# Own tiles for pieces and differences in attention's sums, and one load and one store for the block differences of the token stage

## The chip, the cores and the metric

The kernel runs on one core of a Trainium2 chip. The metric is the device time of one execution in microseconds (us), shown as the median of several runs. A profile of one execution shows what each engine did: PE is TensorE (matmuls), DVE is VectorE, ACT is ScalarE, POOL is GpSimd, and SP is SyncE, which here does nothing but issue transfers. A transfer (a DMA) is issued by an engine's queue in that queue's order and lands some microseconds later.

## The reference

One step of a one-layer encoder in float32, for a prompt of 2048 tokens and a sample of 32 tokens with 1024 cached keys. The input is normalised and modulated to h; one projection gives the columns of two branches; a sparse attention (an indexer picks up to 256 keys for each query) and a gated short convolution are merged by gates and projected:

```python
h = rms_norm(x, norm_g) * (1.0 + scale[:, None, :]) + shift[:, None, :]
proj = h @ w_in
(q, k, v, za, qi, ki, wi, u, bg, cg, zb, ga, gb) = jnp.split(proj, ...)
...
_, idx = lax.top_k(score, topk)          # score: indexer, qi . ki, weighted by wi
o = softmax(q . k[idx] / sqrt(d)) @ v[idx]
a_out = (o * jax.nn.silu(za)) @ w_pa
b_out = (bg * conv3(cg * u) * jax.nn.silu(zb)) @ w_pb
merged = jax.nn.sigmoid(ga) * a_out + jax.nn.sigmoid(gb) * b_out
y = x + gate[:, None, :] * (merged @ w_out)
```

The change touches how h and b (the input of `w_pb`) are stored and differenced; what is computed stays the same.

## The kernel before

Every f32 operand is split in two parts, hi and lo (`split`, L194: hi is a cast on ACT, lo a subtraction on DVE or POOL), and each product is three matmuls. The large products use seven block products in place of eight, on the quadrants of an operand (two halves of its 1024 channels, two halves of its tokens) and on differences of these. The differences are made ahead of time and stored in device memory.

**Token stage** (0 to about 274 us of the profile). `mk_h` normalises and transposes pairs of 128-token tiles, makes h, and stores it to `h_d` (L701). The projections that are needed per token (indexer, k, v; matmuls L813 to L815) run at the same time; their results are stored from ACT's queue. In the second half of the stage the block differences of h are made in 12 pieces, 3 chunks of tokens (352, 352, 336 of a half) by 4 slabs of 128 channels, at the steps listed in `SUMS_AT`. `sums_load` (L710) loads the four quadrants of a piece into a tile `hv` by two transfers (L715), one for each channel half; `block_sums` (L719) makes four differences in place on DVE (L724) and stores them with two transfers to `t_d` (L726). The tile has two buffers. The loads and the differences are kept in program order.

**Feature stage** (about 285 to 1750 us). `b_piece` (L1028) loads four slabs of h from `h_d`, or of differences from `t_d`, into `ev` tiles (L1037, seven buffers) and splits them; `mm` multiplies with the split weights `wo` (L1051 to L1053), which come from `wr` (L988). The indexer's scores (transposes L243 of a query tile `qd` that is loaded by L236 and L237, then matmuls L256, L267, L268 and L287) are woven in.

**Attention** (about 1745 to 2290 us). Blocks of 128 queries run in the order 4, 0, 5, 1, 6, 2, 7, 3, 8 to 15. `qk` makes scores (matmuls L1461 to L1463), masks them on DVE (L1472) and takes the exponential on ACT (L1477); `pv` transposes them (L1498), splits them (tiles `th`, `tl`) and multiplies with v (L1506 to L1508); z is loaded by L1513, multiplied in on DVE (L1515, L1516), and the result is stored by L1521. Keys and values are loaded two tiles at a time as the blocks need them (L1393, tile `in`) and split into `khi`, `klo`, `vhi`, `vlo`; queries by L1433, masks by L1426.

From the fifth block of that order on, **side work** is handed out by `sum_steps` (L1282): 32 pieces of b (load L1295 from `b_d`, four subtractions on POOL L432, store L1308 to `xb_d`), one piece for the sample, and 24 sums of weights (load L1328, four POOL operations L1332, store L1335 to `o_d`). All of them use one tag `wq` of 4 KB per partition with two buffers. A piece of b takes its first half for the input and its second half for the differences:

```python
st["t"] = tile_()
load(st["t"][:, :512].rearrange("p (k t) -> p k t", k=2), ...)
...
o = st["t"][:, 512:].rearrange("p (s b t) -> p s b t", s=4, t=64)
```

The step list issues the load of piece i+1 ahead of the subtractions of piece i. Since a tile is free only when everything that reads it is done, the load of piece i+2 waits until the store of piece i has landed.

What sets the order: nearly all loads and stores are issued by SP, in one in-order queue (`load = store = nc.sync.dma_start`); a transfer whose condition isn't met holds all that are queued behind it. The order of the instructions within each engine is decided by the framework's scheduler when the kernel is built, from program order and priorities, except where `tc.keep_in_program_order` fixes it. Transfers share eight semaphores (lanes) in turn, and a transfer waits, beside its data, for an earlier one on its lane. A pool opened with `reuse_waits="tile"` takes over memory of closed pools with waits for the tiles that lay there, and a pool without it with waits for the engines that used the memory.

Of the kernel before, what the change touches and what calls it, by code (L numbers as in the profile page):

```python
# [9 lines left out]
F32 = mybir.dt.float32  # L10
# [4 lines left out]
ALU = mybir.AluOpType  # L15
# [4 lines left out]
P = 128  # L20
D = 1024
KT = 8
SEQ = 2048
# [3 lines left out]
NTOK = SEQ + NS  # L27
NB = 16
HT = NTOK // 2
CHUNKS = [(0, 352), (352, 352), (704, 336)]  # L30
# [79 lines left out]
def body(ctx, tc, x_prompt, x_sample, cache_k, cache_v, cache_idx_k, state_conv, c_prompt, c_sample,  # L110
# [3 lines left out]
    V, S, G, T = nc.vector, nc.scalar, nc.gpsimd, nc.tensor  # L114
    load = nc.sync.dma_start
    store = nc.sync.dma_start
# [3 lines left out]
    def nm(s):  # L120
        uid[0] += 1
        return f"{s}_{uid[0]}"
# [10 lines left out]
    dp = ctx.enter_context(tc.tile_pool(name="dp", bufs=1, space=DRAM))  # L133
# [13 lines left out]
    c_d = dp.tile([2, D], F32, name="c_d", tag="c_d")  # L147
    ga_d = dp.tile([KT, P, NTOK], F32, name="ga_d", tag="ga_d")
    gb_d = dp.tile([KT, P, NTOK], F32, name="gb_d", tag="gb_d")
    h_d = dp.tile([KT, P, NTOK], F32, name="h_d", tag="h_d")  # L150
    t_d = dp.tile([KT, P, NTOK], F32, name="t_d", tag="t_d")
    s_d = dp.tile([NF, P, 1024], F32, name="s_d", tag="s_d")
    o_d = dp.tile([3, 2, 2, P, 4, 512], F32, name="o_d", tag="o_d")
    u_d = [dp.tile([NF, P, HT], F32, name=f"u_d{i}", tag=f"u_d{i}") for i in range(3)]
# [279 lines left out]
    def sample_pieces(src, dst, to, r0):  # L434

        n = src.shape[-1] // (4 * 16)
        x = src.rearrange("p (r k h t) -> p r k h t", k=2, h=2, t=16)
        o = dst[:, :n * P].rearrange("p (r s t) -> p r s t", s=8, t=16)
        for k in range(2):
            G.tensor_copy(o[:, :, 2 * k:2 * k + 2, :], x[:, :, k, :, :])  # L440
        differences([[x[:, :, k, h, :] for h in range(2)] for k in range(2)], [o[:, :, 4 + i, :] for i in range(4)])
        for r in range(n):
            store(to[r0 + r, :, :, HT - 16:].rearrange("s p t -> p s t"), o[:, r])
# [115 lines left out]
    with ExitStack() as p1:  # L559
# [124 lines left out]
        def mk_h(j):  # L684

            pr, xs = allp[j], xnorm.pop(j)
            tot = sum(n for _, n, _ in pr)
            off = pr[0][2]
            r0 = pr[0][0] * P
            vsel = 0 if pr[0][0] < NB else 1  # L690
            for kt in range(KT):
                pt = pst.tile([P, 512], F32, name=nm("pt"), tag="pt") if kt % 3 < 2 or r0 == 0 else psi.tile([P, 512], F32, name=nm("pt"), tag="pi")
                for i, (t, n, _) in enumerate(pr):
                    T.transpose(pt[:, i * P:i * P + n], xs[i][:n, kt * P:(kt + 1) * P], ident[:n, :n])
                if kt % 2 == 0:
                    f2 = xp.tile([P, 2, 256], F32, name=nm("f"), tag="f", bufs=2)
                f = f2[:, kt % 2, :]
                V.tensor_scalar(f[:, :tot], pt[:, :tot], amod[:, kt, vsel:vsel + 1], bmod[:, kt, vsel:vsel + 1], ALU.mult, ALU.add)
                split(hhi[:, kt, off:off + tot], hlo[:, kt, off:off + tot], f[:, :tot], eng=V if kt % 4 == 0 else G)
                if kt % 2:  # L700
                    store(h_d[kt - 1:kt + 1, :, r0:r0 + tot].rearrange("k p t -> p k t"), f2[:, :, :tot])  # L701
            x_load(j + 2)
            x_norm(j + 1)

        halved = {}

        def both(x, d, c0, tb):

            return x[:, :2 * tb].rearrange("p (h t) -> p h t", h=2), d.rearrange("p (h t) -> p h t", h=2)[:, :, c0:c0 + tb]

        def sums_load(ch, kt):
            t = ip.tile([P, SEQ], F32, name=nm("hv"), tag="sc", bufs=2)
            xs = halved[ch, kt] = t[:, 0:D], t[:, D:2 * D]
            for x, k in zip(xs, (kt, kt + 4)):
                tc.keep_in_program_order(load(*both(x, h_d[k], *CHUNKS[ch])))  # L715

        def block_sums(ch, kt):

            c0, tb = CHUNKS[ch]  # L719
            x1, x2 = halved.pop((ch, kt))  # L720
            a, b = slice(0, tb), slice(tb, 2 * tb)
            for o, p, q in ((x1[:, a], x1[:, b], x1[:, a]), (x1[:, b], x2[:, b], x1[:, b]),
                            (x2[:, b], x2[:, b], x1[:, a]), (x2[:, a], x2[:, a], x2[:, b])):
                tc.keep_in_program_order(V.tensor_tensor(o, p, q, ALU.subtract))  # L724
            for x, k in ((x1, kt), (x2, kt + 4)):
                store(*both(x, t_d[k], c0, tb)[::-1])  # L726

        nw = len(TOK)
        wseq = [c for _, c in TOK] * 2
# [223 lines left out]
    with ExitStack() as p2:  # L953
# [74 lines left out]
        def b_piece(k, ch):  # L1028

            c0, tb = CHUNKS[ch]  # L1030
            src, k0, hf = ((h_d, 0, 0), (t_d, 4, 1), (t_d, 0, 0), (t_d, 0, 1), (h_d, 4, 0), (t_d, 4, 0), (h_d, 4, 1))[k]
            tg = BTAG[k, ch]
            hi = hps[tg > 1].tile([P, 4, TB], F32R, name=nm("bh"), tag=f"bh{tg}")
            lo = hps[tg > 1].tile([P, 4, TB], F32R, name=nm("bl"), tag=f"bl{tg}")
            for kt in range(4):
                r = ev()
                load(r[:, :tb], src[k0 + kt, :, hf * HT + c0:hf * HT + c0 + tb])  # L1037
                split(hi[:, kt, :tb], lo[:, kt, :tb], r[:, :tb])
            bop[k, ch] = (hi, lo)

# [238 lines left out]
    env.small = lambda: ip.tile([P, 512], F32, name=nm("sm"), tag="qd", bufs=2)  # L1279


    def sum_steps(pool):  # L1282

        def tile_():
            return pool.tile([P, 1024], F32, name=nm("wq"), tag="wq", bufs=2)

        def pieces(i):
            r, j = i // 8, i % 8  # L1290
            st = {}

            def get():
                st["t"] = tile_()
                load(st["t"][:, :512].rearrange("p (k t) -> p k t", k=2), b_d[2 * r:2 * r + 2, :, 256 * j:256 * j + 256].rearrange("k p t -> p k t"))  # L1295
                for k in range(2):
                    for h in range(2):
                        if j == 0 and (k, h) != (0, 1):
                            load(xb_d[r, 2 * k + h, :, 0:HT - 16].rearrange("p (b t) -> p b t", t=64),
                                 b_d[2 * r + k, :, 0:SEQ].rearrange("p (b h t) -> p h b t", h=2, t=64)[:, h])  # L1300

            def diff():
                x = st["t"][:, :512].rearrange("p (k b h t) -> p k h b t", k=2, h=2, t=64)
                o = st["t"][:, 512:].rearrange("p (s b t) -> p s b t", s=4, t=64)
                differences([[x[:, k, h] for h in range(2)] for k in range(2)], [o[:, q] for q in range(4)], tc.keep_in_program_order)

            def put():
                store(xb_d[r, 4:8, :, 128 * j:128 * j + 128].rearrange("s p t -> p s t"), st["t"][:, 512:].rearrange("p (s t) -> p s t", s=4))  # L1308

            return get, [(1.9, diff)], put  # L1310

        def sample():
            st = {}

            def get():
                st["t"] = tile_()
                load(st["t"][:, :256].rearrange("p (k t) -> p k t", k=KT), b_d[:, :, SEQ:].rearrange("k p t -> p k t"))

            return get, [(2.5, lambda: sample_pieces(st["t"][:, 0:256], st["t"][:, 512:1024], xb_d, 0))], lambda: None

        def unit(i):
            at = (i // 8, i // 4 % 2, i // 2 % 2)
            cols = slice(256 * (i % 2), 256 * (i % 2) + 256)
            st = {}

            def get():
                st["t"] = tile_()
                load(st["t"].rearrange("p (q c) -> p q c", q=4), w_q[at][:, :, cols])  # L1328

            def add(o, p, q, op):  # L1330
                w = st["t"].rearrange("p (q c) -> p q c", q=4)
# [12 lines left out]
        for i, (_, ops, put) in enumerate(units):  # L1344
            steps += ops
            if i + 1 < len(units):
                steps.insert(len(steps) - len(ops), (0.0, units[i + 1][0]))
            steps.append((0.0, put))
        return steps

    def attention(shared=None, aside=()):
        aside = list(aside)
        sums = []
        with ExitStack() as p2:
# [52 lines left out]
                split(vhi[:, j:j + 2, :], vlo[:, j:j + 2, :], vt.rearrange("p (j c) -> p j c", j=2))  # L1407

            if shared:
                sums = sum_steps(p2.enter_context(tc.tile_pool(name="wq", bufs=1)))  # L1410
            count = [0]
            turn = [0]

# [608 lines left out]
```

## Time and profile before

| what | value |
| --- | --- |
| median of 3 runs | 2814.1 us (2812.35, 2814.1, 2817.15) |
| the profiled execution | 2817.44 us |
| its span in the profile | 2815.5 us |
| mean granted clock of PE | 0.992 |
| token stage, to the last token product | 0 to 274 us |
| feature stage | about 285 to 1750 us |
| attention | about 1745 to 2290 us |
| outputs (feature steps L1768, token steps L1838) | from about 2270 us |

The span is what the profiler saw of the program; the device time of the same execution is 1.9 us longer. A row such as `engine line op out<-in xcount` names an instruction by its engine, its line in the kernel, what it writes and reads. A timeline row has its start and its duration in us in front, and in brackets the idle time ahead of it and what ended that. A row of SP is the issue of a transfer; the duration there is that of the issue, not that of the transfer. In a row of windows a mean clock of 1.00 is full speed.

### The profile page before, as it was taken

What the parts mean: (1) busy time and instruction counts of PE and PEld (TensorE: products, weight loads), DVE (VectorE), ACT (ScalarE), POOL (GpSimd) and SP (SyncE); (2) the same over time, 40 slices, a digit from 0 to 9 for tenths busy, and PEclk for the clock granted to TensorE, in tenths of its full rate; (3) what the DMA queues carried; (4) which work ended last, traced back from release to release, by engine and by line L of the source; (5) the groups of instructions that cost most, each with busy time, mean ns of one, the idle gap of its engine ahead of it and who ended that gap; (6) DMA issues with size and microseconds to landing.
All of it is one profiled execution on the core that took longest, in us unless ns stands there. A gap on an engine that the chain in (4) does not pass through costs nothing. (4 is left out here: it accounts for less than half of the span.)

```text
span 2815.5 us, 51671 instructions
## 1 busy us (share of the span) xinstructions
PE 2724.2 (97%) x18184; PEld 2636.6 (94%) x18184; DVE 2164.2 (77%) x4531; ACT 1502.0 (53%) x2701; POOL 1029.9 (37%) x1430
## 2 busy tenths in 40 slices
PE   8998999999999999999999999999999999999998
PEld 6988899999999999999999999889899999999997
DVE  6666747577777888788778866888887778887988
ACT  4433655666666764434554433675665655444553
POOL 3342645455564234222342221667544430010100
PEclk9999899999999999999999999999999999999999
DMA  8578755445455676555766675666654469896885
GB/s 293 183 245 271 232 170 177 158 159 174 161 174 164 223 211 223 177 182 186 260 212 215 213 238 169 147 178 184 166 161 136 129 222 346 235 307 206 266 284 154
DMA packets 485841, 576.29 MB, mean 205 GB/s; under 512 B 179506, under 2 KB 375298, under 8 KB 484546
## 3 DMA queue, kind: packets, MB, share of 16 engines
q1 hardware_dynamic: 462594, 546.96, 61.9%
q10 hardware_dynamic: 18816, 13.85, 1.5%
q0 software_dynamic: 4160, 12.06, 1.2%
q8 instruction: 145, 2.38, 0.4%
q14 instruction: 126, 1.03, 0.1%
HBM read 379.83 MB, written 199.22 MB: 206 GB/s over the span
## 5 line engine op out<-in xcount | busy, mean ns | idle before, releaser
L1051 PE MATMUL pm<-bh,wo 128*128 128x352 f32 (+1 forms) x2688 | 865.0, 323 | 9.5 <-DVE u L1150 5.7
L1052 PE MATMUL pm<-bl,wo 128*128 128x352 f32 (+1 forms) x2688 | 863.5, 321 | 0.0
L1053 PE MATMUL pm<-bh,wo 128*128 128x352 f32 (+1 forms) x2688 | 861.6, 322 | 0.0
L1051 PEld LDWEIGHTS pm<-bh,wo 128*128 128x128 f32 x2688 | 506.6, 189 | 18.4 <-DVE u L1150 6.4
L1052 PEld LDWEIGHTS pm<-bl,wo 128*128 128x128 f32 x2688 | 507.4, 189 | 6.0 <-issue 1.0
L1053 PEld LDWEIGHTS pm<-bh,wo 128*128 128x128 f32 x2688 | 505.7, 188 | 3.7 <-POOL ws L1000 0.7
L197 POOL TENSOR_TENSOR wo<-wr,wo 128x512 fp32r<-128x512 f32 x160 | 222.3, 1390 | 635.4 <-ACT wo L196 605.9
L293 DVE SCALAR_TENSOR_TENSOR sc<-pi,wi,sc 128x384 f32<-128x384 f32 (+2 forms) x266 | 180.1, 680 | 64.6 <-ACT pi L289 61.4
L289 ACT ACTIVATE pi<-pi 128x512 f32<-128x512 f32 (+2 forms) x304 | 157.2, 527 | 134.9 <-PE pi L288 131.0
L1594 ACT CAST wh<-rw 128x1024 fp32r<-128x1024 f32 x128 | 134.1, 1052 | 171.6 <-PE ps L1769 78.7
L196 ACT CAST th<-pt 128x512 fp32r<-128x512 f32 (+1 forms) x288 | 153.5, 560 | 123.9 <-PE pt L1498 113.4
L1768 PE MATMUL ps<-xh,wh 128*128 128x384 f32 (+1 forms) x672 | 214.2, 321 | 2.2 <-ACT oa L1723 0.9
L1769 PE MATMUL ps<-xl,wh 128*128 128x384 f32 (+1 forms) x672 | 214.4, 320 | 0.0
L1770 PE MATMUL ps<-xh,wl 128*128 128x384 f32 (+1 forms) x672 | 211.9, 320 | 0.5 <-DVE wl L1595 0.5
L197 DVE TENSOR_TENSOR tl<-pt,th 128x512 fp32r<-128x512 f32 (+1 forms) x288 | 183.9, 655 | 36.9 <-ACT th L196 36.1
L1595 DVE TENSOR_TENSOR wl<-rw,wh 128x1024 fp32r<-128x1024 f32 x128 | 156.0, 1225 | 53.8 <-ACT wh L1594 53.6
L1477 ACT ACTIVATE s<-s,sc,rts 128x640 f32<-128x640 f32 (+15 forms) x128 | 166.0, 1297 | 50.0 <-DVE sc L1476 43.0
L196 ACT CAST wo<-wr 128x512 fp32r<-128x512 f32 x160 | 98.6, 616 | 150.1 <-PE pm L1052 105.4
L1849 POOL DMA_DIRECT2D out_dram<-om x60 | 31.6, 533 | 392.4 <-DVE om L1847 392.4
L367 ACT ACTIVATE low<-sc,w 32x1056 f32<-32x1056 f32 (+14 forms) x105 | 136.5, 1300 | 55.7 <-DVE w L372 55.6
L1506 PE MATMUL po<-th,vhi 128*128 128x256 f32 x544 | 159.4, 293 | 5.8 <-ACT th L196 3.5
L1498 PE MATMUL pt<-ident,s 128*128 128x128 f32 x1088 | 157.8, 274 | 3.3 <-ACT s L1477 2.1
(331 smaller groups left out, 7148.4 us busy)
## 6 DMA issues: line engine op xcount, KB each, us to landing
u<-u_d SPq DMA_DIRECT2D x128, 520.0 KB, 4.1
wr<-in_w_f_dram SPq DMA_DIRECT2D x96, 512.0 KB, 4.1
rw<-o_d SPq DMA_DIRECT2D x72, 512.0 KB, 7.1
u_d<-ev SPq DMA_DIRECT2D x192, 176.0 KB, 2.5
rw<-in_w_q_dram SPq DMA_DIRECT2D x56, 512.0 KB, 5.4
s_d<-ws SPq DMA_DIRECT2D x64, 256.0 KB, 2.6
wr<-s_d SPq DMA_DIRECT2D x32, 512.0 KB, 4.6
xa_d<-a SPq DMA_DIRECT2D x64, 256.0 KB, 3.6
```

What stands on the lines that cost most here:

```text
L196: S.copy(hi, src)
L197: (eng or V).tensor_tensor(lo, src, hi.bitcast(F32), ALU.subtract)
L293: V.scalar_tensor_tensor(sc[:n, o:o + w], pi[:n, :w], wi[:n, b, h:h + 1], sc[:n, o:o + w], ALU.mult, ALU.add)
L1051: T.matmul(ps[:, :tb], wh[:, kt, :], bh[:, kt, :tb], start=(first and kt == 0), stop=False, **more)
L1052: T.matmul(ps[:, :tb], wh[:, kt, :], bl[:, kt, :tb], start=False, stop=False, **more)
L1053: T.matmul(ps[:, :tb], wl[:, kt, :], bh[:, kt, :tb], start=False, stop=(kt == 3), **more)
L1477: S.activation(sm[:, :L], sm[:, :L], AF.Exp, bias=sc[:, 16 + i:17 + i], scale=r, accum_out=sc[:, 18 + i:19 + i])
L1498: T.transpose(pt[:, (2 * jj + i) * P:(2 * jj + i + 1) * P], sms[i][:, j * P:(j + 1) * P], ident)
L1506: T.matmul(po[:, 0:256], vh_, th[:, pc], start=(j == 0), stop=False)
L1768: T.matmul(ps[:, :tb], wh[:, kt, wc], xh[:, kt, :tb], start=(first and kt == 0), stop=False, **more)
L1769: T.matmul(ps[:, :tb], wh[:, kt, wc], xl[:, kt, :tb], start=False, stop=False, **more)
L1770: T.matmul(ps[:, :tb], wl[:, kt, wc], xh[:, kt, :tb], start=False, stop=(kt == 3), **more)
```

## The change

There are two parts. In the token stage, `h_d` is laid out by slab of channels, so that a slab's two channel halves lie next to each other for each partition; `t_d` becomes three tensors, one for each chunk of tokens, with the four differences of a slab in one run. One load and one store then serve each piece of differences. In attention, the input and the differences of a piece have tiles of their own (`wi` and `wo`, 2 KB per partition and two buffers each); the sums of weights take whole tiles of 4 KB, as before, from a second pool, which is opened when the first of them is asked for, after the first has been closed. Both pools are opened with `reuse_waits="tile"`. The number of instructions of PE, DVE, ACT and POOL is the same; SP issues 24 transfers fewer, all in the token stage.

```diff
-    h_d = dp.tile([KT, P, NTOK], F32, name="h_d", tag="h_d")
-    t_d = dp.tile([KT, P, NTOK], F32, name="t_d", tag="t_d")
+    h_d = dp.tile([4, P, 2, NTOK], F32, name="h_d", tag="h_d")
+    t_d = [dp.tile([4, P, 4, tb], F32, name=f"t_d{ch}", tag=f"t_d{ch}") for ch, (_, tb) in enumerate(CHUNKS)]
...
-                    store(h_d[kt - 1:kt + 1, :, r0:r0 + tot].rearrange("k p t -> p k t"), f2[:, :, :tot])
+                    m = (kt - 1) % 4
+                    store(h_d[m:m + 2, :, kt // 4, r0:r0 + tot].rearrange("k p t -> p k t"), f2[:, :, :tot])
...
             t = ip.tile([P, SEQ], F32, name=nm("hv"), tag="sc", bufs=2)
-            xs = halved[ch, kt] = t[:, 0:D], t[:, D:2 * D]
-            for x, k in zip(xs, (kt, kt + 4)):
-                tc.keep_in_program_order(load(*both(x, h_d[k], *CHUNKS[ch])))
+            c0, tb = CHUNKS[ch]
+            x = halved[ch, kt] = t[:, :4 * tb].rearrange("p (q t) -> p q t", q=4)
+            tc.keep_in_program_order(load(x, h_d[kt].rearrange("p k (h t) -> p (k h) t", h=2)[:, :, c0:c0 + tb]))
...
-            for o, p, q in ((x1[:, a], x1[:, b], x1[:, a]), (x1[:, b], x2[:, b], x1[:, b]),
-                            (x2[:, b], x2[:, b], x1[:, a]), (x2[:, a], x2[:, a], x2[:, b])):
-                tc.keep_in_program_order(V.tensor_tensor(o, p, q, ALU.subtract))
-            for x, k in ((x1, kt), (x2, kt + 4)):
-                store(*both(x, t_d[k], c0, tb)[::-1])
+            x = halved.pop((ch, kt))
+            for o, p, q in ((0, 1, 0), (1, 3, 1), (3, 3, 0), (2, 2, 3)):
+                tc.keep_in_program_order(V.tensor_tensor(x[:, o], x[:, p], x[:, q], ALU.subtract))
+            store(t_d[ch][kt], x)
...
-                load(r[:, :tb], src[k0 + kt, :, hf * HT + c0:hf * HT + c0 + tb])
+                load(r[:, :tb], src[ch][kt, :, k0 // 2 + hf, :] if src is t_d else src[kt, :, k0 // 4, hf * HT + c0:hf * HT + c0 + tb])
...
-    def sum_steps(pool):
+    def sum_steps(pools):
+        held = {"pool": pools.enter_context(tc.tile_pool(name="wq", bufs=1, reuse_waits="tile"))}
+
+        def half_():
+            return [held["pool"].tile([P, 512], F32, name=nm(t), tag=t, bufs=2) for t in ("wi", "wo")]
 
         def tile_():
-            return pool.tile([P, 1024], F32, name=nm("wq"), tag="wq", bufs=2)
+            if "whole" not in held:
+                pools.close()
+                held["pool"] = held["whole"] = pools.enter_context(tc.tile_pool(name="wu", bufs=1, reuse_waits="tile"))
+            return held["pool"].tile([P, 1024], F32, name=nm("wq"), tag="wq", bufs=2)
...
-                st["t"] = tile_()
-                load(st["t"][:, :512].rearrange("p (k t) -> p k t", k=2), ...)
+                st["t"] = half_()
+                load(st["t"][0].rearrange("p (k t) -> p k t", k=2), ...)
...
-                store(xb_d[r, 4:8, ...], st["t"][:, 512:].rearrange("p (s t) -> p s t", s=4))
+                store(xb_d[r, 4:8, ...], st["t"][1].rearrange("p (s t) -> p s t", s=4))
...
-                sums = sum_steps(p2.enter_context(tc.tile_pool(name="wq", bufs=1)))
+                sums = sum_steps(p2.enter_context(ExitStack()))
```

SP's queue in attention, ahead of the second load of v (keys 8 and 9, for block 8; the rows give line, transfer and shape). Before:

```order
L1308 DMA xb_d<-wq_21577 128x4x128
L1513 DMA z_22029<-z_d 128x2x128
L1295 DMA wq_21879<-b_d 128x2x256
L1393 DMA in_22711<-v_d 128x2x256
L1521 DMA xa_d<-a_21780 128x8x64
```

After the change, the same place (lines moved by one):

```order
L1309 DMA xb_d<-wo_21561 128x4x128
L1296 DMA wi_21864<-b_d 128x2x256
L1394 DMA in_22706<-v_d 128x2x256
L1514 DMA z_22016<-z_d 128x2x128
L1522 DMA xa_d<-a_21765 128x8x64
```

The load of z stands behind the load of v now, and not ahead of the piece load.

SP's queue at the end of the token stage, from the last load of `hv` to the second load of the sample's `qd`. Before:

```order
L715 DMA hv_3563<-h_d 128x2x336 x2
L726 DMA t_d<-hv_3425 256x1x336
L1037 DMA ev_3900<-h_d 128x352
L1037 DMA ev_3904<-h_d 128x352
L1037 DMA ev_3908<-h_d 128x352
L726 DMA t_d<-hv_3563 256x1x336
L1037 DMA ev_3912<-h_d 128x352
L726 DMA t_d<-hv_3563 256x1x336
...
L1037 DMA ev_3976<-t_d 128x352
L237 DMA qd_4189<-qi_d 32x4x64
L988 DMA wr_3890<-in_w_f_dram 128x1024
```

After the change:

```order
L719 DMA t_d_78<-hv_3266 128x1344
L1030 DMA ev_3878<-h_d 128x352
L1030 DMA ev_3882<-h_d 128x352
L712 DMA hv_3544<-h_d 128x4x336
L1030 DMA ev_3886<-h_d 128x352
L1030 DMA ev_3890<-h_d 128x352
L719 DMA t_d_78<-hv_3408 128x1344
...
L1030 DMA ev_3924<-h_d 128x336
L719 DMA t_d_78<-hv_3544 128x1344
L236 DMA qd_4167<-qi_d 32x4x64
...
L237 DMA qd_4167<-qi_d 32x4x64
```

The last `hv` load stands behind two loads of `ev`, and the last store behind nine, where before the last two stores had three and four of them ahead. Ahead of L237 there are 13 loads of `ev` in place of 15.

PE behind the transposes of that `qd`, before:

```order
L243 MATMUL pt_4194<-ident,qd_4189 128x32 x4
L256 MATMUL pt_4203<-ident,sm_4201 128x32 x2
L267 MATMUL pi_4229<-kiS,qh_4110 128x352
L268 MATMUL pi_4229<-kiS,ql_4111 128x352
L1051 MATMUL pm_4082<-bh_3898,wo_3894 128x352
L1052 MATMUL pm_4082<-bl_3899,wo_3894 128x352
```

After the change:

```order
L243 MATMUL pt_4172<-ident,qd_4167 128x32 x4
L1044 MATMUL pm_4060<-bh_3876,wo_3872 128x352
L1045 MATMUL pm_4060<-bl_3877,wo_3872 128x352
L1044 MATMUL pm_4097<-bh_3894,wo_3872 128x352
L1045 MATMUL pm_4097<-bl_3895,wo_3872 128x352
L1044 MATMUL pm_4113<-bh_3922,wo_3872 128x336
L1045 MATMUL pm_4113<-bl_3923,wo_3872 128x336
L256 MATMUL pt_4181<-ident,sm_4179 128x32 x2
L267 MATMUL pi_4207<-kiS,qh_4088 128x352
```

The first six products of the feature stage stand ahead of the sample's index products.

More of the change, by code (lines that the diff above doesn't have):

```diff
@@ L705, in body @@
         halved = {}
-        def both(x, d, c0, tb):
-            return x[:, :2 * tb].rearrange("p (h t) -> p h t", h=2), d.rearrange("p (h t) -> p h t", h=2)[:, :, c0:c0 + tb]
         def sums_load(ch, kt):
             t = ip.tile([P, SEQ], F32, name=nm("hv"), tag="sc", bufs=2)
-            xs = halved[ch, kt] = t[:, 0:D], t[:, D:2 * D]
-            for x, k in zip(xs, (kt, kt + 4)):
-                tc.keep_in_program_order(load(*both(x, h_d[k], *CHUNKS[ch])))
+            c0, tb = CHUNKS[ch]
+            x = halved[ch, kt] = t[:, :4 * tb].rearrange("p (q t) -> p q t", q=4)
+            tc.keep_in_program_order(load(x, h_d[kt].rearrange("p k (h t) -> p (k h) t", h=2)[:, :, c0:c0 + tb]))
         def block_sums(ch, kt):
-            c0, tb = CHUNKS[ch]
-            x1, x2 = halved.pop((ch, kt))
-            a, b = slice(0, tb), slice(tb, 2 * tb)
-            for o, p, q in ((x1[:, a], x1[:, b], x1[:, a]), (x1[:, b], x2[:, b], x1[:, b]),
-                            (x2[:, b], x2[:, b], x1[:, a]), (x2[:, a], x2[:, a], x2[:, b])):
-                tc.keep_in_program_order(V.tensor_tensor(o, p, q, ALU.subtract))
-            for x, k in ((x1, kt), (x2, kt + 4)):
-                store(*both(x, t_d[k], c0, tb)[::-1])
+            x = halved.pop((ch, kt))
+            for o, p, q in ((0, 1, 0), (1, 3, 1), (3, 3, 0), (2, 2, 3)):
+                tc.keep_in_program_order(V.tensor_tensor(x[:, o], x[:, p], x[:, q], ALU.subtract))
+            store(t_d[ch][kt], x)
         nw = len(TOK)
@@ L1293, in get @@
             def get():
-                st["t"] = tile_()
-                load(st["t"][:, :512].rearrange("p (k t) -> p k t", k=2), b_d[2 * r:2 * r + 2, :, 256 * j:256 * j + 256].rearrange("k p t -> p k t"))
+                st["t"] = half_()
+                load(st["t"][0].rearrange("p (k t) -> p k t", k=2), b_d[2 * r:2 * r + 2, :, 256 * j:256 * j + 256].rearrange("k p t -> p k t"))
                 for k in range(2):
@@ L1302, in diff @@
             def diff():
-                x = st["t"][:, :512].rearrange("p (k b h t) -> p k h b t", k=2, h=2, t=64)
-                o = st["t"][:, 512:].rearrange("p (s b t) -> p s b t", s=4, t=64)
+                x = st["t"][0].rearrange("p (k b h t) -> p k h b t", k=2, h=2, t=64)
+                o = st["t"][1].rearrange("p (s b t) -> p s b t", s=4, t=64)
                 differences([[x[:, k, h] for h in range(2)] for k in range(2)], [o[:, q] for q in range(4)], tc.keep_in_program_order)
             def put():
-                store(xb_d[r, 4:8, :, 128 * j:128 * j + 128].rearrange("s p t -> p s t"), st["t"][:, 512:].rearrange("p (s t) -> p s t", s=4))
+                store(xb_d[r, 4:8, :, 128 * j:128 * j + 128].rearrange("s p t -> p s t"), st["t"][1].rearrange("p (s t) -> p s t", s=4))
             return get, [(1.9, diff)], put
@@ L1315, in get @@
             def get():
-                st["t"] = tile_()
-                load(st["t"][:, :256].rearrange("p (k t) -> p k t", k=KT), b_d[:, :, SEQ:].rearrange("k p t -> p k t"))
-            return get, [(2.5, lambda: sample_pieces(st["t"][:, 0:256], st["t"][:, 512:1024], xb_d, 0))], lambda: None
+                st["t"] = half_()
+                load(st["t"][0][:, :256].rearrange("p (k t) -> p k t", k=KT), b_d[:, :, SEQ:].rearrange("k p t -> p k t"))
+            return get, [(2.5, lambda: sample_pieces(st["t"][0][:, 0:256], st["t"][1], xb_d, 0))], lambda: None
         def unit(i):
```

## The prediction, made before the change was run

> **What bounds the kernel now.** I read the page's first part, then TensorE's (PE's) waits, then windows of the stages which the change touches, then SP's waits and the timelines of single stalls.
>
> ```profile
> PE 2724.2 (97%) x18184; PEld 2636.6 (94%) x18184; DVE 2164.2 (77%) x4531; ACT 1502.0 (53%) x2701; POOL 1029.9 (37%) x1430
> ```
>
> PE is busy for 2724.2 of 2815.5 us and the change neither adds nor removes a matmul. So the time can fall only by part of the 91.3 us in which PE is idle, and by the stretches in which it runs at a low clock. Where does it wait, in the stages touched?
>
> ```profile
> PE ps L1461 <- DVE sc L1472: 12.5, 9, 2.9
> ```
>
> The columns are us in total, times, and the longest. In attention the score products wait for VectorE's (DVE's) mask step, 9 times, 12.5 us; a single stall of 7.31 us, quoted below, stands where the token stage ends. Windows (PE, PEld, DVE, ACT, POOL busy; then clock, DMA share, GB/s):
>
> ```profile
> 140.00:210.00 70.00, 66.25 (x490) 62.64 (x489) 48.65 (x140) 26.34 (x70) 29.62 (x48) 1.00 0.77 243
> 210.00:240.00 30.00, 27.95 (x227) 26.22 (x227) 21.39 (x79) 13.53 (x50) 9.59 (x18) 1.00 0.71 229
> 240.00:270.00 30.00, 29.16 (x254) 28.66 (x253) 18.93 (x79) 6.68 (x30) 4.76 (x10) 1.00 0.91 297
> 281.00:291.00 10.00, 7.41 (x29) 5.77 (x30) 4.66 (x7) 5.44 (x14) 5.56 (x5) 0.60 0.93 297
> 1862.00:1867.00 5.00, 5.00 (x21) 4.04 (x20) 4.17 (x13) 2.87 (x6) 2.35 (x6) 0.66 0.45 122
> 1763.00:1768.00 5.00, 5.00 (x27) 4.88 (x27) 4.12 (x14) 3.16 (x8) 1.47 (x4) 0.66 0.35 101
> ```
>
> In the half of the token stage where the block differences run (140 to 270 us) PE lacks 3.75 + 2.05 + 0.84 = 6.6 us: that is all that a better load or store there can return. After a stall the clock falls: a 5 us window at a mean of 0.66 has lost 5 x 0.34 = 1.7 us of work.
>
> SP is one in-order queue for nearly all transfers, so what its head waits for holds everything behind it. Its waits from 1650 to 2310 us:
>
> ```profile
> SPq L1513 <- DVE a L1516: 78.7, 25, 9.0
> SPq L1295 <- DMA xb_d<-wq: 67.8, 29, 5.0
> ```
>
> The second row is the wait that the change takes away: the load of a piece (L1295) stands at SP's head until the store of the piece two before has landed.
>
> **The change, part by part.** *Attention's sums.* Same loads, POOL subtractions and stores; only L1295's wait for the landing goes. POOL's own work on the pieces is on no chain to PE. What counts is what stood behind L1295 on SP. The clearest place:
>
> ```profile
> 1851.20 0.36 SPq L1308 DMA_DIRECT2D xb_d<-wq  x1
> 1853.14 0.36 SPq L1513 DMA_DIRECT2D z<-z_d  x1
> 1855.36 0.36 SPq L1295 DMA_DIRECT2D wq<-b_d  x1
> 1855.78 0.46 SPq L1393 DMA_DIRECT2D in<-v_d  x1
> ```
> ```profile
> 1858.92 0.62 ACT L196 CAST vhi<-in 128x512 fp32r<-128x512 f32 x1 [3.90 <-DMA in<-v_d]
> ```
> ```profile
> 1859.57 0.88 DVE L197 TENSOR_TENSOR vlo<-in,vhi 128x512 fp32r<-128x512 f32 x1 [2.43 <-ACT vhi L196]
> ```
> ```profile
> 1861.65 0.50 PE L1461 MATMUL ps<-khi,qh 128*128 128x512 f32 x1 [2.36 <-DVE sc L1472]
> ```
>
> Read downwards, this is one chain: L1295 goes out 4.16 us after the store, the load of v right behind it; ScalarE (ACT) waits 3.90 us for v, DVE 2.43 for ACT, and PE 2.36 because DVE's mask step stands behind the split. In the new order store, piece load and v load follow one another, with z behind, so v is asked for at about 1852.0 instead of 1855.78: 3.8 us earlier, more than PE's stall. I take the stall and its low clock whole: 2.36 + 1.7 = **4.0 us** (from 0 to 4.1).
>
> The next two loads of v:
>
> ```profile
> 1904.54 0.48 SPq L1513 DMA_DIRECT2D z<-z_d  x1
> 1906.67 0.36 SPq L1295 DMA_DIRECT2D wq<-b_d  x1
> ```
> ```profile
> 1915.71 0.45 PE L1461 MATMUL ps<-khi,qh 128*128 128x384 f32 x1 [2.76 <-DVE sc L1472]
> ```
> ```profile
> 1983.29 0.42 SPq L1308 DMA_DIRECT2D xb_d<-wq  x1
> 1986.71 0.36 SPq L1295 DMA_DIRECT2D wq<-b_d  x1
> ```
> ```profile
> 1992.43 0.87 PE L1498 MATMUL pt<-ident,s 128*128 128x128 f32 x6 [2.07 <-ACT s L1477]
> ...
> 1994.95 0.39 PE L1506 MATMUL po<-th,vhi 128*128 128x256 f32 x1 [0.79 <-ACT th L196]
> ```
>
> At the first of them L1295 held the queue for 1906.67 - 1905.02 = 1.65 us, and a mask load, a store and a table stand between it and v. PE's 2.76 us shrink by **1.6** (0 to 3.3: with 1.1 us left of the stall the clock might hold too, 1.7 more as in the windows above). At the second the hold is 3.0 us against stalls of 2.07 + 0.79 = 2.86; there a mask load now stands ahead of v, and PE waits for an exponential on ACT with more work of its own, so I take half, **1.4** (0 to 2.9).
>
> Attention's first loads:
>
> ```profile
> 1750.18 0.37 SPq L1426 DMA_DIRECT2D mk<-m_d  x1
> 1753.14 0.88 SPq L1295 DMA_DIRECT2D wq<-b_d  x2
> ...
> 1755.60 1.78 SPq L1433 DMA_DIRECT2D in<-q_d  x2
> ```
> ```profile
> 1762.79 0.41 PE L1461 MATMUL ps<-khi,qh 128*128 128x384 f32 x1 [2.88 <-DVE sc L1472]
> ```
>
> SP sits for 2.6 us ahead of the first two piece loads, which before waited for PE and ACT as well as for lanes, because their memory belonged to pools closed just before; with the new pool they wait for lanes alone. The q loads behind them still wait for a DVE split, so at most 1.6 us of the 2.88 can go (3.3 with the clock); half of it, **0.8** (0 to 3.3). The weights' sums that follow use whole tiles as before, and their waits stay. All in all 4.0 + 1.6 + 1.4 + 0.8 = **7.8 us less** (0 to 13.6).
>
> A low clock behind stalls of 2.4 to 2.9 us carries 1.7 of this. The Trainium skill (TensorE: Matmul & The Clock Gate, Part 1: The HAM clock gate) halves the clock after an idle window of some 3.4 us that runs freely. Stalls this short would by that rule mostly leave the clock alone, and the term would be 6.1 us; the windows at 0.66 behind such stalls say otherwise, and the sum goes by them.
>
> *Token stage.* Where 24 loads and 24 stores ran there are 12 and 12; the DVE operations are the same 48.
>
> ```profile
> L715 SPq DMA_DIRECT2D hv<-h_d x24: 519/580/775, 151.3 to 258.1; - x24
> ...
> DMA to landing us min/median/max: 3.5/4.8/5.7
> ```
> ```profile
> L726 SPq DMA_DIRECT2D t_d<-hv x24: 513/555/1741, 166.9 to 266.8; - x24
> ...
> DMA to landing us min/median/max: 2.7/3.3/4.1
> ```
>
> SP saves 12 x 0.58 + 12 x 0.56 = 13.7 us of issuing, spread over 115 us, and cannot return more than the 6.6 us above. Against it, the first difference waits for 704 KB and not for 352, and the store leaves after the fourth difference and not after the second. Nothing of this size is in the trace; the nearest row is the load of 352 KB at 4.8 us, and a pair of them, one behind the other, had both landed by 4.8 + 0.58 = 5.4. So the first difference can come up to 0.6 us later, the last one sooner. The first load goes out at 151.3 and the loads run ahead of their use by several us, which covers this; without that cover it is 12 x 0.6 = 7 us on DVE, which is busy 48.65 of 70 us there and can take in about half of it. I take **0** (6.6 less to 4 more).
>
> The skill (DMA: Bandwidth & Descriptors, Rules for kernel authors) advises merging small transfers since a share of each is fixed; its fit, 2.0 us + bytes/436e3, gives an estimated 3.7 us for the merged load and a small gain here. The row of 4.8 us for half the bytes, in a stage whose DMA share reaches 0.91, speaks against counting on it.
>
> *The end of the token stage.* Rows of SP and PE:
>
> ```profile
> 274.07 2.14 SPq L1037 DMA_DIRECT2D ev<-h_d  x2
> 276.30 1.34 SPq L1037 DMA_DIRECT2D ev<-t_d  x3
> 277.90 0.34 SPq L237 DMA_DIRECT2D qd<-qi_d  x1
> ```
> ```profile
> 281.58 0.60 PE L243 MATMUL pt<-ident,qd 32*128 32x32 f32 x4 [7.31 <-DMA qd<-qi_d]
> ```
>
> PE waits for the second load of qd, which stands on SP behind 15 loads of ev and the last stores of t_d. In the new order 13 loads of ev stand ahead of it, one store less and one load of hv among them, and the first products come before the index products. Two loads fewer at the rate of the ev rows here (2.14 / 2 and 1.34 / 3, so 0.4 to 1.1 us each) are 0.9 to 2.1 us, a store less 0.6. The stall cannot go beyond 7.31 us plus the low clock after it, 7.41 busy x (1 - 0.60) = 3.0, together 10; and the hv load, now behind two loads of ev that wait for split buffers, can hold the last store and the qd load by some 4 us. I take **2 less** (10 less to 4 more).
>
> *Sum:* -7.8 + 0 - 2 = -9.8. The profiled execution took 2817.4 us (2815.5 of span and 1.9 around it), so 2807.6; it stands 3.3 us above the median of the three runs, 2814.1, and from that median the forecast is **2804.3 us**.
>
> **Rivals.** *The freed time is taken back.* The wait of 67.8 us is in SP's queue and not on PE. SP's own larger row, z behind DVE (78.7 us), takes over its head, and v comes hardly sooner. For it: z loads stand all among the pieces, and DVE is busy for 4.17 of the 5 us after the second stall. Against it: in the new order z stands behind v at the costliest place. With a quarter of the attention term and nothing elsewhere: -2 us, 2812.
>
> *The merged load makes the token stage later.* The differences are held in program order on DVE, so one that waits holds the rope, normalisation and split work behind it, and PE's transposes behind that. Four of the pairs wait today, 1.55 us each in the mean:
>
> ```profile
> DVE hv L724 <- DMA hv<-h_d: 6.2, 4, 2.6
> ```
>
> If all 12 waited 1.55, that is 18.6 - 6.2 = 12.4 us more on DVE; with half of it passed on to PE and 4 us more at the last store and the qd load, +10, against -4 from attention: about 2820. It decides from the point where a load lands about 1 us after DVE reaches its difference, in most of the 12. Against it: the first load goes out 14 us before its difference (151.3 to 165.6).
>
> *The qd load arrives in time.* If qd is there when PE ends the token products, the whole 10 us of stall and clock go: -7.8 - 10, 2796. Against it: a DMA share of 0.93 in that window and 13 loads still ahead.
>
> *The change does not do what it says:* the piece load could still be held, by a lane or by its own tile's last reader on POOL. Then attention stays, and the time is that of the first rival.
>
> **How the numbers follow.** The forecast, between 2800 and 2809: 0.45. The freed time taken back, or the wait kept, 2809 to 2818: 0.30. Later token stage, 2818 to 2825: 0.12. The qd load in time, 2793 to 2800: 0.13. The range leaves out about half of each end case: 2796 to 2818, which the bounds of attention (0 to 13.6) fill with little from the other terms. A measurement of this kernel can tell about 0.2%, 5.6 us, from no change, so faster is below 2808.5: 0.13 + 0.42 = 0.55; slower is above 2819.7: 0.11; within: 0.34.
>
> **What would show it.** Right: the row of L1295 behind xb_d is gone from SP's waits or below 10 us; ACT's waits for v (3.90, 4.89, 7.38 us before the casts named above) are each shorter by 1.5 us or more; the PE row behind DVE's L1472 falls from 12.5 to under 8; the clock beside 1862 stays at 1.00. For the token stage: PE's busy time in 140 to 270 within 2 us, the waits of DVE for hv not above 10 us, and the stall for qd between 4 and 7 us. Wrong: z's wait grows by what L1295's loses; the hv waits come 12 times; a stall of PE that is new stands in the first 30 us of the feature stage, or attention starts late although every stall named here is gone.

## The result, and the profile after

The changed kernel takes 2799.29 us (median of 6 runs, 2795.2 to 2803.34) where the kernel before takes 2816.99 us in its 6 runs there: a ratio of 0.9944 with a 95% interval of 0.9933 to 0.9954, 13 to 19 us less. It lies within the range, 2796 to 2818; the gain by the ratio, 15.8 us, is 1.6 times the 9.8 us that were forecast. On a second chip the same kernel gave 0.9950 (0.9936 to 0.9963). Two single executions, of 3811 us (`a1_tiles` below) and of 5418 us (`t2_store`), are left out of the ratios in this document.

The first part of the page, PE's waits over the whole span (us in total, times, longest), and SP's and ACT's waits in attention, all of the changed kernel:

```profile
PE 2718.9 (97%) x18184; PEld 2632.8 (94%) x18184; DVE 2162.4 (77%) x4531; ACT 1502.4 (54%) x2701; POOL 1030.0 (37%) x1430
```
```profile
PE pm L1044 <- ACT wo L196: 5.4, 1, 5.4
PE ps L1462 <- DVE sc L1473: 5.3, 8, 2.5
...
PE pt L243 <- DMA qd<-qi_d: 0.6, 1, 0.6
```
```profile
SPq L1514 <- DVE a L1517: 99.2, 37, 9.0
```
```profile
ACT vhi L196 <- DMA in<-v_d: 8.7, 4, 3.8
```

PE idles 77.3 us of the span in place of 91.3. The wait for the mask step (L1472 before, L1473 now) has fallen from 12.5 to 5.3 us, the wait for `qd` from 7.31 to 0.6; the wait for split weights `wo` has grown from 1.6 us to 5.4. On SP there is no row left of a piece load behind `xb_d`; the wait of z behind DVE has grown from 78.7 to 99.2 us. ACT's wait for v was this before:

```profile
ACT vhi L196 <- DMA in<-v_d: 19.0, 5, 7.4
```

The place that the prediction followed down four engines, after the change (timeline of SP, then of ACT):

```profile
1840.73 0.36 SPq L1309 DMA_DIRECT2D xb_d<-wo  x1
1841.43 0.36 SPq L1296 DMA_DIRECT2D wi<-b_d  x1
1841.89 0.44 SPq L1394 DMA_DIRECT2D in<-v_d  x1
1843.41 0.36 SPq L1514 DMA_DIRECT2D z<-z_d  x1
```
```profile
1845.57 0.62 ACT L196 CAST vhi<-in 128x512 fp32r<-128x512 f32 x1 [1.93 <-DMA in<-v_d]
```

v is asked for 1.16 us after the store; before, it was 4.58. ACT still waits 1.93 us for it, but PE has no stall behind it. Windows of PE, PEld, DVE, ACT, POOL busy, clock, DMA share and GB/s, at attention's start, behind that load, and over most of the blocks with side work:

```profile
1740.00:1765.00 25.00, 19.61 (x129) 18.93 (x130) 20.58 (x78) 16.41 (x38) 9.61 (x25) 0.86 0.53 154
1845.00:1870.00 25.00, 24.93 (x162) 21.83 (x161) 23.98 (x64) 18.96 (x36) 18.00 (x45) 1.00 0.67 178
1765.00:2000.00 235.00, 227.58 (x1641) 212.84 (x1641) 206.10 (x569) 156.69 (x301) 166.50 (x421) 1.00 0.70 181
```

Before, the first and the last of these, at the same distance from attention's start to within 0.4 us, were:

```profile
1750.00:1775.00 25.00, 19.30 (x128) 18.53 (x127) 20.78 (x76) 16.52 (x38) 9.12 (x23) 0.86 0.53 157
1775.00:2010.00 235.00, 221.08 (x1577) 206.35 (x1576) 199.55 (x552) 150.32 (x289) 158.45 (x406) 0.99 0.67 172
```

PE does 6.5 us more of its work in the 235 us, at a full clock. At attention's start little has changed: PE is busy for 19.6 us in place of 19.3, and the clock is 0.86 in both.

The end of the token stage, timelines of SP and of PE of the changed kernel:

```profile
272.86 0.32 SPq L237 DMA_DIRECT2D qd<-qi_d  x1
...
276.25 2.34 SPq L981 DMA_DIRECT2D wr<-in_w_f_dram  x2
```
```profile
276.15 0.40 PE L243 MATMUL pt<-ident,qd 32*128 32x32 f32 x4 [0.58 <-DMA qd<-qi_d]
281.98 0.66 PE L1044 MATMUL pm<-bh,wo 128*128 128x352 f32 x1 [5.43 <-ACT wo L196]
```

`qd` is there in time, and PE goes on waiting, now for the first weights: their loads `wr` go out at 276.25, and the first product starts 5.73 us later.

### The profile page after: what moved, and what is told of

Read it like the earlier page. It is cut to its first block, busy times and chain, and to the rows that moved or that the text cites. A ratio compares the mean times of both kernels' runs of the same rounds, so it can differ in the third digit from the quotient of the medians.

```text
span 2796.2 us, 51624 instructions
## 1 busy us (share of the span) xinstructions
PE 2718.9 (97%) x18184; PEld 2632.8 (94%) x18184; DVE 2162.4 (77%) x4531; ACT 1502.4 (54%) x2701; POOL 1030.0 (37%) x1430
## 3 DMA queue, kind: packets, MB, share of 16 engines
q8 instruction: 145, 2.38, 0.4%
```

## The experiments

Each kernel was timed against the kernel before on the same chip; ratios are to that, with 95% intervals. The kernel before takes 2814 to 2817 us there, so 0.001 is 2.8 us. Since single profiled executions differ by some us, marks are read over all of them: when the first `wr` of the feature stage is issued, the start of the first recorded feature product (L1051), of the 65th, of the last, and of the last L1516 of attention.

| kernel | one store | own tiles | wr issued | first | 65th | last | attention (last product to last L1516) | ratio |
| --- | --- | --- | --- | --- | --- | --- | --- | --- |
| before | | | 278.33 | 285.3 | 336.1 | 1747.4 | 559.1 | 1 |
| q_early | | | 279.69 | 286.5 | 336.2 | 1745.9 | 553.2 | 1.0000 |
| t3_chunks | | | 277.22 | 282.9 | 333.4 | 1745.1 | 555.4 | 0.9987 |
| t1_load | | | 279.68 | 285.4 | 334.8 | 1744.9 | 564.0 | 1.0013 |
| a2_pool | | | 277.37 | 283.0 | 334.8 | 1747.6 | 563.3 | 1.0000 |
| p2_attn | | yes | 278.17 | 284.0 | 334.6 | 1741.7 | 549.3 | 0.9974 |
| a1_tiles | | yes | 279.33 | 285.0 | 336.0 | 1749.3 | 549.3 | 0.9959 |
| p1_token | yes | | 275.28 | 280.8 | 326.6 | 1734.4 | 559.2 | 0.9984 |
| t2_store | yes | | 277.07 | 283.5 | 329.4 | 1739.4 | 559.0 | 0.9979 |
| t2_attn | yes | yes | 275.09 | 281.6 | 328.1 | 1739.9 | 552.5 | 0.9951 |
| changed | yes | yes | 276.25 | 282.0 | 328.8 | 1737.1 | 552.4 | 0.9944 |
| after_again | yes | yes | 274.77 | 280.7 | 326.2 | 1738.5 | 551.6 | 0.9950 |
| z_pool | yes | yes | 274.12 | 280.2 | 325.9 | 1735.2 | 560.0 | 0.9961 |

Two columns part without overlap. With one store the 65th product starts at 325.9 to 329.4 us, otherwise at 333.4 to 336.2: means 327.5 and 335.1, 7.6 us. With own tiles attention takes 549.3 to 552.5 us (leaving out `z_pool`), otherwise 553.2 to 564.0: means 551.0 and 559.0, 8.0 us. Between the same two marks PE is idle for 16.8 to 18.4 us with own tiles and for 21.9 to 27.0 without, 6.4 us less in the mean; the rest is clock.

**The two parts, each alone.** `p1_token` undoes attention's part, `p2_attn` the token stage's:

```diff
-                sums = sum_steps(p2.enter_context(ExitStack()))
+                sums = sum_steps(p2.enter_context(tc.tile_pool(name="wq", bufs=1)))
...
```

> The token stage's part alone; attention's sums as before. Theory (the two parts add): the last feature product moves by about 10 us, as it did in the changed kernel (1747.4 to 1737.1), and attention keeps its length and its stalls behind v, so the time falls by about 10 us (ratio 0.9963). Rival (the 4 us that were gained between 830 and 1030 us of the feature stage were an accident of that execution): the last feature product moves by 6 us only, ratio 0.998. Second rival (attention gains from its earlier start alone): the whole 17 us, ratio 0.994.

> Attention's part alone; token stage as before. Theory (the two parts add, and attention's gain is v asked for earlier): everything up to 1745 us stays within 1 us of before, ACT's waits for v fall from 19 us to below 10, attention ends 8 to 10 us sooner, ratio 0.9967. Rival (the gain of attention needs the other part): within 3 us of before.

The first gives 0.9984 (0.9974 to 0.9994), 4.5 us where its theory had about 10, and so comes nearest to its first rival's 0.998. The second gives 0.9974 (0.9963 to 0.9986), which takes in its forecast. Their product is 0.9958, and the whole change's intervals reach to 0.9954 and 0.9963: the parts add within the error. ACT's wait for v tells them apart, `p1_token` first, then `p2_attn`:

```profile
ACT vhi L196 <- DMA in<-v_d: 20.6, 5, 7.0
```
```profile
ACT vhi L196 <- DMA in<-v_d: 8.4, 4, 2.9
```

That `p2_attn` also has its last product at 1741.7, with the same instructions as before up to there, and not within 1 us of before, is how far one execution can be off. The profiled executions of these two took 2801.7 and 2797.6 us, where their kernels' medians are 2807.9 and 2805.5: their marks show them 6 and 8 us better than a typical run.

**Own tiles or the pool's waits?** `a1_tiles` keeps the tiles and drops `reuse_waits`, with the token stage of before; `a2_pool` is the kernel before with `reuse_waits` alone:

```diff
-        held = {"pool": pools.enter_context(tc.tile_pool(name="wq", bufs=1, reuse_waits="tile"))}
+        held = {"pool": pools.enter_context(tc.tile_pool(name="wq", bufs=1))}
...
-                sums = sum_steps(p2.enter_context(tc.tile_pool(name="wq", bufs=1)))
+                sums = sum_steps(p2.enter_context(tc.tile_pool(name="wq", bufs=1, reuse_waits="tile")))
```

> Attention's part with the own tiles alone; both pools opened without reuse_waits, so the first piece loads still wait for the engines. Token stage as before. Theory (the landing wait behind which v stood is the cause): the row of L1295 behind xb_d goes, ACT's waits for v fall from 18 to 21 us to below 10, and 6 us or more of the 7.3 us of attention's part are there: ratio 0.9970 to 0.9980. Rival (the pools' waits at attention's start are the cause): within 0.1% of before.

> The other half of attention's part: one tile for input and differences as before, but its pool opened with reuse_waits. Theory: the row of L1295 behind xb_d stays at 60 to 70 us, ACT's waits for v at 17 us or more, and at most the 1 to 2 us of attention's first loads are gained: ratio 0.9993 to 1.0005. Rival: 0.9975, as attention's part.

0.9959 (0.9943 to 0.9975) and 1.0000 (0.9988 to 1.0013): the tiles are all of it. In `a2_pool` SP's row stays:

```profile
SPq L1295 <- DMA xb_d<-wq: 65.0, 29, 5.0
```

**Does PE wait for qd?** `q_early` moves two loads in the kernel before:

```diff
-            load(qd[:n, :, 0, :], src)
-            load(qd[:n, :, 1, :], src)
+            with tc.high_priority(300 if smp else 0):
+                load(qd[:n, :, 0, :], src)
+                load(qd[:n, :, 1, :], src)
```

> The kernel before, with one thing moved: the two loads of the sample's second query tile qd stand on SP behind 4 loads of ev, not behind 15; the first load of wr stays where it was. Theory of the prediction (PE's 7.3 us wait for qd is what delays the feature stage): the first feature product comes 3 to 7 us sooner than 285.3, and the time falls by as much. Rival (the first product waits for wr, whose load stands behind the same 18 transfers; the wait for qd only covers it): the wait for qd goes, a wait for the split weights wo of 4 to 6 us takes its place, the first product stays within 1 us of 285.3 and the time within 3 us.

1.0000 (0.9990 to 1.0011). PE's and DVE's timelines of it:

```profile
282.92 0.42 PE L257 MATMUL pt<-ident,sm 32*128 32x32 f32 x2 [7.11 <-DVE ql L197]
...
286.45 0.66 PE L1052 MATMUL pm<-bh,wo 128*128 128x352 f32 x1 [1.26 <-ACT wo L196]
```
```profile
280.78 1.76 DVE L197 TENSOR_TENSOR bl<-ev,bh 128x336 fp32r<-128x336 f32 x4 [1.18 <-ACT bh L196]
282.57 0.49 DVE L197 TENSOR_TENSOR ql<-pt,qh 128x128 fp32r<-128x128 f32 x2
```

The wait for `qd` is gone, and one of 7.11 us stands in its place: the split of the query (`ql`) is queued on DVE behind splits of h (`bl`), which wait for their loads. This is the rival's outcome (time and first product stay, the product to 1.1 us), though not by the weights alone, as the rival had it. And in every kernel of the table the first product comes 5.5 to 7.0 us after `wr` is issued. The stall of 7.31 us covered that wait. The changed kernel's two profiles say the same: PE waits 0.58 us for `qd` in the first and 4.16 in the second, and the first product comes at 282.0 and at 280.7.

**Load or store?** `t1_load` keeps the merged load and stores in two as before; `t2_store` keeps the merged store and loads in two; `t3_chunks` is the kernel before with only the differences' tensor split in three:

```diff
-            store(t_d[ch][kt], x)
+            for s, k in ((0, kt), (2, kt + 4)):
+                store(t_d[k].rearrange("p (h t) -> p h t", h=2)[:, :, c0:c0 + tb], x[:, s:s + 2])
...
-            tc.keep_in_program_order(load(x, h_d[kt].rearrange("p k (h t) -> p (k h) t", h=2)[:, :, c0:c0 + tb]))
+            for s, k in ((0, kt), (2, kt + 4)):
+                tc.keep_in_program_order(load(x[:, s:s + 2], h_d[k].rearrange("p (h t) -> p h t", h=2)[:, :, c0:c0 + tb]))
...
-                store(*both(x, t_d[k], c0, tb)[::-1])
+                store(t_d[ch][k], x[:, :2 * tb].rearrange("p (h t) -> p h t", h=2))
```

> Token stage with the one load for each piece alone (h_d in its new layout); two stores into the old t_d; attention as before. SP issues 12 transfers fewer, wr stands behind 17 loads of ev, 4 after qd, and index and product matmuls are spread among each other as in the changed kernel. Theory (what counts is the place of wr on SP and the spread of index matmuls among products): no stall of 3.9 us at the first index scores of block 16, and the first 64 products end 5 us or more sooner than 336: ratio 0.9980. Rival (load and store each bring half of the part): first product 1.5 us sooner, ratio 0.9992.

> Token stage with the one store for each piece alone (three t_d tensors); two loads from h_d in its old layout; attention as before. SP issues 12 transfers fewer; ahead of wr stand 13 loads of ev and then 4 more around qd, and index scores of block 15 stand more closely together among the products than in the changed kernel. Theory (the store is the part's gain and the load its cost, since the load alone was 0.13% slower and split chunks alone 0.13% faster): ratio 0.9965 to 0.9985, DVE's waits for hv near 6 us as before and not 10. Rival (the transition's order as a whole makes the gain, by the one or the other): first 64 products end at 334 us or later, ratio 0.9990 to 1.0005.

> The kernel before with the differences' tensor t_d alone split into three, one per chunk; still two loads and two stores for each piece, and no instruction changes its place. Theory (what moved was the order of SP's queue, not a wait for other chunks' stores): within 3 us of before, first feature product within 1 us of 285.3. Rival (loads of differences waited for the stores of all chunks): first product and time 2 to 4 us sooner.

`t1_load` 1.0013 (1.0004 to 1.0022), `t2_store` 0.9979 (0.9968 to 0.9989), `t3_chunks` 0.9987 (0.9978 to 0.9997). The number of `ev` loads ahead of `wr` is 15 in each, not 17 as two expectations have it. The load alone brings nothing: `wr` stays at 279.68, and both of its expectations are missed. `t2_store` brings the part's whole gain. But it also splits the differences' tensor in three, as `t3_chunks` does, which has no instruction in another place and by the theory should not have gained: it gains 0.8 to 6 us. Its outcome is nearer to its rival's, a first product 2.5 us sooner (282.9), though `a2_pool`, with the token stage of before, has it at 283.0 too. Its stores take as short an issue (0.33 us at the median) as the merged ones (0.34), and like those they write one run for each partition, not two. Why that helps was not followed further; how much of `t2_store`'s gain is the single store and how much the split tensor isn't shown.

**Does the load cost anything in the whole?** `t2_attn` is the changed kernel with the two loads of before.

> The same together with attention's part: the changed kernel without its merged load. Theory (the load costs): faster than the changed kernel on the same chip by 0.05 to 0.2%. Rival (the order at the transition is worth more than the load costs): slower than it by 0.1% or more, first 64 products at 334 us or later against 326 to 329.

> The changed kernel once more, on the chip of the two others. The parts alone gave 0.9984 and 0.9974 (0.9959 for the own tiles alone), together some 0.996 to 0.9945. Theory (the parts add): 0.994 to 0.996, first 64 products at 325 to 329 us, ACT's waits for v below 10 us. Rival (the first ratio, 0.9944, was high for its chip): 0.996 to 0.998.

0.9951 (0.9937 to 0.9964) and 0.9950 on one chip: not measurably. DVE's wait for `hv` was 10.0 us in the changed kernel's first profile, 4.5 in the second and 5.5 in `t2_attn`, so it differs as much between executions as between the kernels.

**Does z hold the rest?** `z_pool` is the changed kernel with one queue exchanged:

```diff
-                    load(z.rearrange("p (h q) -> p h q", h=2), z_d[hs, :, r0:r0 + P].rearrange("h p t -> p h t"))
+                    G.dma_start(z.rearrange("p (h q) -> p h q", h=2), z_d[hs, :, r0:r0 + P].rearrange("h p t -> p h t"))
```

> The changed kernel with attention's loads of z issued from POOL's queue and not SP's, where their wait for DVE is now the largest (99 us). Theory (SP's queue no longer sets anything: PE waits only some 10 us in attention, for DVE and ACT): within 0.15% of the changed kernel, ratio 0.993 to 0.996 against before. Rival (z took over the head of SP's queue and keeps part of the gain): 3 to 6 us faster than the changed kernel, ratio 0.9925. Second rival (a wait of z at POOL's head holds the products' diagonal and the piece sums): slower than the changed kernel by 5 us or more, 0.996 and above.

0.9961 (0.9948 to 0.9973). The interval takes in the changed kernel's 0.9950, but the value is the second rival's, and in the profile attention takes 560.0 us, with PE idle for 23.3 us of it: as much as without own tiles. Nor did the wait leave SP. The stores of the result (L1522) now stand there for the same step of DVE (the changed kernel, then `z_pool`):

```profile
SPq L1522 <- DVE a L1517: 15.7, 3, 8.0
```
```profile
SPq L1522 <- DVE a L1517: 82.8, 20, 7.8
```

And POOL has waits of its own in that execution, which now stand ahead of the loads of z:

```profile
POOL dg L1492 <- PE po L1511: 75.8, 32, 10.0
POOL a L1519 <- DVE a L1517: 54.0, 27, 8.3
```

So this run does not show what the wait for z on SP is worth; it shows that moving its loads to POOL does not help.

## Why the prediction was right, and where it was not

**Attention, 7.8 us forecast: right.** Its marks give 8.0 us; the part alone 3.9 to 10.4 us, the tiles alone 7 to 16. The cause is the one named: the tiles carry it, the piece load no longer waits for the landing of `xb_d`, and v is asked for sooner. Of the 7.8 us, 6.1 were stalls and 1.7 low clock; the idle time of PE fell by 6.4 us. By terms: the 4.0 us at the second load of v came whole, stall and clock (1.00 from 1845 to 1870). At the third load 1.1 us of PE's 2.76 were to be left, and 1.04 are, behind DVE's splits, which follow v:

```profile
1899.44 0.63 PE L1499 MATMUL pt<-ident,s 128*128 128x128 f32 x4 [1.04 <-DVE tl L197]
```

In the second profile of the changed kernel it is 2.38 us there. ACT's wait for v at this load fell only from 4.89 to 3.85 us, less than the 1.5 us that were named as a sign; at the second load it fell from 3.90 to 1.93. At the fourth ACT does not wait for v at all, and the term of 1.4 us, half of two stalls, was cut too cautiously. At attention's start, 0.8 us forecast, PE's stall of 2.88 us is now one of 2.14 for another step (ACT's `th`), but nothing of that reaches further: the last product is followed by the first L1516 after 23.6 us before and 23.5 now. That the pool's waits are worth nothing measurable is shown by `a2_pool`.

Two things limit this. Every variant was scheduled anew, and with own tiles the load of z also stands behind v, so the landing and the new order were not taken apart. And waits alone are no measure: in `t2_store`, without own tiles, ACT waits 11.0 us for v (19.0 before) and PE 5.6 for the mask step (12.5 before), yet attention takes 559.0 us, with PE idle for 23.2.

**Token stage, 0: right.** The last token product ends at 273.9 us in the mean of the seven kernels with two stores and at 272.7 in the six with one. In the changed kernel's own profile PE is busy for 121.5 us from 140 to 270, 123.4 before, within the 2 us that were named. The estimate of 3.7 us for the merged load has no row here to be held against, and the fit behind it is stated by the Trainium skill (DMA: Bandwidth & Descriptors, Anatomy of one DMA — SWDGE (gpsimd) path) for transfers issued from GpSimd; these go out from SP.

**The end of the token stage, 2 us forecast: the step that failed.** It was worth 7.6 us at the 65th product; about 1 us of that is order alone, since with one store up to six index matmuls fewer stand ahead of that product. At the 3000th recorded matmul of PE, the index matmuls counted in, the difference is 6.7 us. The prediction took PE's wait for `qd` as the thing that delays the feature stage, counted two `ev` loads and a store less ahead of it, and allowed at most 10 us. `q_early` shows that loading `qd` sooner gains nothing. The stall for `qd`, forecast at 4 to 7 us, was 0.58 us in one profile and 4.16 in the other, and what grew there was PE's wait for the weights, 1.60 us before and 5.43 now. Two other things moved:

- The first weights. `wr` goes out at a mean of 278.5 us with two stores and at 275.4 with one, 3.1 us sooner, and the first product starts 3.1 us sooner (284.6 and 281.5). In the kernel before `wr` stood directly behind the second `qd` load, issued at 277.90, when PE had long ended its token products. What to count was the path to `wr`.
- The index scores of block 15. From the first to the 65th product it takes 50.5 us with two stores and 46.0 with one, 4.5 us. In the kernel before stood this stall, with a low clock behind it, and in the changed kernel there is none (PE's timeline of before, then the window from 300 to 330 us of before and of the changed kernel):

```profile
310.82 0.80 PE L287 MATMUL pi<-kiT,qh 128*128 128x512 f32 x1 [3.92 <-DVE sc L293]
```
```profile
300.00:330.00 30.00, 26.08 (x139) 24.37 (x138) 21.01 (x45) 22.27 (x47) 19.93 (x19) 0.89 0.74 241
```
```profile
300.00:330.00 30.00, 30.00 (x180) 28.26 (x179) 18.59 (x41) 22.45 (x46) 22.08 (x21) 1.00 0.76 250
```

The order of PE shows why it can go. A score is two matmuls (L287, L288), and the scores have three buffers in all (`pst` has two, L542, `psi` one, L543), so a fourth waits until DVE has taken an earlier one out. The table gives where the scores' first matmuls stand, counted from 0 over all recorded matmuls of PE, and PE's waits ahead of them:

| kernel | places of the first scores of block 15 | PE waits |
| --- | --- | --- |
| before | 2013, 2019, 2041, 2043, 2045, 2047 | 3.92 us ahead of 2047 |
| t1_load | 2017, 2039, 2041, 2055, 2057 | 1.23 us ahead of 2055, 2.14 ahead of 2057 |
| t2_store | 2037, 2039, 2041, 2079, 2081, 2083 | none |
| changed | 2013, 2039, 2077, 2079, 2117 | none |

In each of the seven kernels with two stores five or six scores stand within 41 matmuls, and PE waits 3.4 to 5.1 us among them; in each of the six with one store no more than three do, and it waits for none. The two effects come apart: `t2_store`, `t3_chunks` and `a2_pool` issue `wr` within 0.3 us of each other, and `t2_store` is still 4.0 and 5.4 us ahead of the others at the 65th product.

The prediction read the rows up to 291 us and never priced this stall, although it said that PE's order would move. The stall of 3.92 us at 310 us is in that profile's waits, and its low clock too. That the spreading removes it is read from order and profile; no run moved the index scores alone.

**The rivals.** SP's head was indeed taken over by z, by 20 us of the 68, but attention gained what was forecast without a term for that, and PE's waits for the step that takes z in (L1517) are 1.7 us in total, 2.2 before. What is left to gain from z isn't known, since `z_pool` did not take the wait off SP. The merged load does cost something alone (0.04 to 0.22%, 1 to 6 us, by its runs), less than the 10 us of that rival, and nothing measurable in the whole. The time of 2799 lies in the band of the rival in which `qd` arrives in time (2793 to 2800, chance 0.13), but not by its mechanism: the stall turned into the one for `wo`. That the total still lies so near is luck.

**What stays open.** The token stage's part is 8.6 us by the marks at the last feature product and only 1.7 to 7.3 us by its runs (`t2_store` 3.1 to 9.0). Which of the two is nearer, what the split tensor has of it, and why two stores in place of one send `wr` out later while the number of loads ahead is the same, wasn't settled. That single executions were profiled does not explain it: in the mean those with two stores took 2.1 us less than their kernels' medians, those with one 1.8. Each variant was scheduled anew, so transfers and order could not be separated.

## What to carry to other kernels

When an in-order queue waits for a landing, look at what stands behind it and not at the wait's sum: 68 us of SP's wait were worth 8, because three loads of v stood there. A run that is to price such a wait has to take it off the queue: with the loads of z on another queue, the next transfer stood there for the same step. Give the input and the output of a load, compute and store step tiles of their own, so that the next load waits for the computation and not for the landing. Where a few buffers are shared, count how close together their users stand: five or six scores within 41 matmuls stalled PE on three buffers, three did not. A stall's releaser is only the last to arrive; before pricing it, ask what the engine would wait for next (here the weights), and when the build moves instructions, price every stall in the stretch that moved.

## What was not expected of the hardware

Near the end of the token stage the DMA engines are nearly always busy: the window of `q_early` from 270 to 290 us has a DMA share of 0.94 at 310 GB/s, and asking earlier for a small load did not bring the first product sooner (286.5, before 285.3).

```profile
270.00:290.00 20.00, 11.59 (x70) 9.07 (x69) 8.24 (x21) 9.67 (x28) 3.44 (x3) 0.69 0.94 310
```

A store that is twice as large is issued faster and lands hardly later, where its runs lie together in memory. The rows are the store's and its landing in the changed kernel; before, at the median, its issue took 555 ns and it landed after 3.3 us. In `t3_chunks`, where the size is that of before and the runs lie together, these are 332 ns and 2.6 us:

```profile
L719 SPq DMA_DIRECT2D t_d<-hv x12: 319/339/418, 167.5 to 266.8; - x12
...
DMA to landing us min/median/max: 3.2/3.5/3.9
```
